# Attention masks of three branches added by identity products on TensorE, for the first half of layer 0

## The chip, the cores and the metric

The kernel runs on one core of a Trainium2 chip. The metric is device time in microseconds of one launch of the whole program, as a median of several runs. The engines are named as in the profile: PE is TensorE's matmuls, PEld its weight loads, DVE is VectorE, ACT is ScalarE, POOL is GpSimd, SP issues the DMAs.

## The reference, cut to what matters

A trunk of two layers works on 1024 tokens of width 1024. Layer 0 mixes the tokens with a sparse attention in three branches (compressed keys, selected keys, a window of 512) and with a grouped attention over a window of 128; layer 1 has a dilated attention. Each layer ends in a gated feed-forward block. All attentions are causal, and what a query may not see is masked before the softmax:

```python
s = jnp.einsum('bhgqd,bhkd->bhgqk', qr_b, kw) * SCALE
s = jnp.where(wmask, s, -jnp.inf)
o_win = jnp.einsum('bhgqk,bhkd->bhgqd', jax.nn.softmax(s, axis=-1), vw)
```

With 16 blocks chosen out of 16, the selected branch sees every key up to the query.

## The kernel before

**Stages.** The program is one long static order for each engine. The dense work (projections, output and feed-forward products) is a list of jobs over tokens 0 to 511 and 512 to 1023; the attentions of each half and layer are lists of units that are threaded between the dense products. This gives four phases of attention: layer 0 first half, layer 0 second half, layer 1 first and second half. The change touches the first of the four; in it each of 8 heads has a branch of kind `B` (window 128), `A` (selected) and `W` (window 512), and one of kind `cmp`.

**The order.** `run` (L377) is a list scheduler written out in the kernel: every task tells which engine it wants next, the task that could start earliest by a modelled clock of each engine goes first, and ties go by priority. `account` (L295) holds the modelled costs. So an operation that is left out moves everything behind it, as far as the modelled clocks move. `attend` (L1868) holds the units back to the pace of the dense work, and lets one through early where the dense product would have to wait.

**A unit.** `s_issue` (L1534) and `maxima` (L1555) first find each query's greatest score: PE products into a bank `pS`, a masked maximum on DVE (an instruction with the mask `mB` or `mW` and an accumulator read), the maxima `MR`, a transpose of `MR` on PE, a copy by ACT to `NM`, and a DMA that puts the row under the query tile. Then `st_unit` (L1613) makes the scores again, transposed, in a bank `pT` (two of these banks exist): for each block of keys two products with four-byte operands, of the same width, in one accumulation. `weights` (L1678) adds the masks on DVE (`pT<-pT,tDE`), takes the exponential on ACT (`S<-pT`), copies it to 16 bits on ACT (`PH<-S`), and subtracts the copy on DVE or POOL to get the low part (`PH<-S,PH`). `pv_unit` (L1700) multiplies both parts with the values (`pO<-S,PH`).

**Which masks.** `mask_ops` (L1640) returns the DVE additions of a unit. A head of kind `B` has two units, of 512 and 384 columns, with three additions (512, 256 and 128 columns); a head of kind `A` or `W` has three units with three additions (128, 256 and 128 columns). `tDE` holds the two triangles, `identB` a 128x128 identity, both in 16 bits. `st_unit` already has the other way, which the setting `ADD` (L58) switches on for each half by the letters of the kinds:

```python
nc.tensor.matmul(st.t[0:kp, o:o + w], a, qa, start=True, stop=False)
if br.get("add"):
    for x, _, kind in br["maskT"](j, bl):
        nc.tensor.matmul(st.t[:, o + x:o + x + P], self.identB, self.tDE[:, kind], start=False, stop=False)
nc.tensor.matmul(st.t[0:kp, o:o + w], b, qb, start=False, stop=True)
```

and `mask_ops` begins with `if br.get("add"): return []`. Every matmul goes through one helper, so the profile gives nearly all work the line L242, and the tiles tell it apart.

Of the kernel before, what the change touches and what calls it, by code (L numbers as in the profile page):

```python
# [54 lines left out]
BEGIN = 700.0  # L55
LEAD = 12000.0
PACE = (0.94, (0.0, 0.85), (0.0, 0.95), (0.0, 0.95))
ADD = ('', '')  # L58
STORE = 1
MM = 213.0  # L60

# [197 lines left out]
class Kernel:  # L259
# [1696 lines left out]
    def branches0(self, h):  # L1956
# [46 lines left out]
        for br in brs:  # L2003
            br["add"] = br["kind"] in ADD[h]
        if h == 0:
# [690 lines left out]
```

## Time and profile before

| | |
|---|---|
| median of 3 runs | 2660.91 us (2660.48 to 2662.5) |
| the profiled execution | 2661.24 us |
| its span, first to last instruction | 2659.2 us |
| PE busy in the span | 2555.7 us (96%) |
| DVE busy | 1882.5 us (71%) |
| ACT busy | 1356.3 us (51%) |
| POOL busy | 728.1 us (27%) |

The span is 2.0 us shorter than the time of that execution, and that execution 0.3 us longer than the median. PE is busy almost without a gap from 500 us on; what idle time it has lies ahead of that. A time that PE saves in the first 500 us is therefore saved at the end, since behind it the order is a queue of products, and a product that is added anywhere is paid at the end unless it fits into a gap.

### The profile page before, as it was taken

The numbers are of one execution on the slowest core, as the hardware profiler recorded it, in microseconds if no ns is written. First come the engines' busy times: TensorE is split into PE (matmuls) and PEld (weight loads), VectorE is DVE, ScalarE is ACT, GpSimd is POOL, SyncE is SP. The second block draws the span as 40 slices with busy tenths as digits, with TensorE's granted clock in tenths as the row PEclk, the third lists the DMA queues.
The fourth block names the chain that finished last, engine by engine and source line by source line (L and its number), as shares of the span: only waits on it lengthen the run. The fifth ranks groups of instructions, "written<-read, shape, count | busy, mean of one in ns | idle before, by whom it ended". The sixth has DMA issues, their size and how long they took to land. (4 is left out here: it accounts for less than half of the span.)

```text
span 2659.2 us, 42231 instructions
## 1 busy us (share of the span) xinstructions
PE 2555.7 (96%) x15446; PEld 1712.2 (64%) x15446; DVE 1882.5 (71%) x4266; ACT 1356.3 (51%) x2303; POOL 728.1 (27%) x513
## 2 busy tenths in 40 slices
PE   8988889999999999999999999999999999999998
PEld 7767768655555688765555688776666667654445
DVE  6888988877777775586666576687777775655554
ACT  7456555566666554344444454355556555433332
POOL 4444643210111446540000345341011114500002
PEclk9989999999999999999999999999999999999999
DMA  8665574233432345834444457954555544533320
GB/s 242 208 175 151 161 243 143 68 100 101 109 99 76 100 149 172 251 93 123 115 123 123 133 170 201 247 146 110 142 147 148 133 124 131 175 106 100 103 71 33
DMA packets 445939, 368.71 MB, mean 139 GB/s; under 512 B 54182, under 2 KB 383782, under 8 KB 445732
## 3 DMA queue, kind: packets, MB, share of 16 engines
q1 hardware_dynamic: 445732, 366.01, 48.7%
q8 instruction: 122, 2.00, 0.3%
q14 instruction: 85, 0.70, 0.1%
HBM read 298.80 MB, written 62.68 MB: 136 GB/s over the span
## 5 line engine op out<-in xcount | busy, mean ns | idle before, releaser
L242 PE MATMUL pD<-S,S 128*128 128x512 f16 (+3 forms) x9648 | 2177.5, 378 | 22.6 <-DVE S L242 15.9
L242 PEld LDWEIGHTS <-S 128*128 128x128 f16 x5376 | 509.3, 100 | 586.0 <-issue 42.3
L242 PEld LDWEIGHTS pD<-S,S 128*128 128x128 f32 x4272 | 729.3, 191 | 140.7 <-DVE S L242 5.8
L242 POOL TENSOR_TENSOR S<-S,S 128x512 f32<-128x512 f32 (+3 forms) x279 | 516.4, 1864 | 839.7 <-ACT S L242 716.4
L242 ACT ACTIVATE S<-pT 128x512 f32<-128x512 f32 (+3 forms) x304 | 171.6, 566 | 356.7 <-DVE pT L242 321.3
L242 ACT CAST S<-S 128x512 fp32r<-128x512 f32 (+2 forms) x283 | 274.1, 1020 | 154.9 <-DVE S L242 59.7
L242 DVE SCALAR_TENSOR_TENSOR S<-S,wsc,S 128x1024 f16<-128x1024 f32 x224 | 298.8, 1334 | 63.1 <-ACT S L242 62.3
L242 ACT ACTIVATE S<-S 128x1024 f16<-128x1024 f32 (+3 forms) x269 | 210.8, 784 | 142.5 <-DVE S L242 137.8
L242 ACT ACTIVATE S<-S,wsc 128x1024 f16<-128x1024 f32 x224 | 253.7, 1142 | 53.8 <-DVE wsc L242 48.5
L242 DVE TENSOR_TENSOR S<-S,S 128x512 fp32r<-128x512 f32 (+4 forms) x163 | 221.7, 1370 | 57.3 <-ACT S L242 55.1
L242 PE MATMUL pT<-S,S 128*128 128x128 f32 (+11 forms) x1072 | 255.1, 365 | 6.0 <-DMA S<-NM 3.6
L242 DVE SCALAR_TENSOR_TENSOR S<-pD,SM,S 128x512 f32<-128x512 f32 x208 | 156.2, 751 | 139.9 <-PE pD L242 130.3
L242 DVE TENSOR_TENSOR S<-pD,S 128x512 f32<-128x512 f32 (+1 forms) x238 | 156.5, 666 | 109.0 <-PE pD L242 90.8
L242 PEld LDWEIGHTS pT<-S,S 128*128 128x128 f32 (+2 forms) x1072 | 202.7, 230 | 35.9 <-DMA S<-NM 4.9
L242 DVE TENSOR_TENSOR PH<-S,PH 128x512 f16<-128x512 f32 (+3 forms) x235 | 173.6, 741 | 39.5 <-ACT PH L242 37.8
L242 POOL TENSOR_TENSOR PH<-S,PH 128x512 f16<-128x512 f32 (+2 forms) x69 | 83.4, 1210 | 418.8 <-ACT PH L242 338.3
L242 ACT ACTIVATE S<-pD,SM 128x512 f32<-128x512 f32 (+2 forms) x136 | 80.6, 605 | 200.8 <-PE pD L242 176.8
L242 ACT CAST PH<-S 128x512 f16<-128x512 f32 (+3 forms) x304 | 177.2, 587 | 10.5 <-PE pO L242 3.0
L242 PEld LDWEIGHTS <-PH 128*128 128x128 f16 (+1 forms) x3384 | 123.5, 99 | 52.8 <-issue 20.1
L242 DVE TENSOR_TENSOR pT<-pT,S 128x128 f32<-128x128 f32 (+4 forms) x176 | 91.8, 525 | 78.3 <-PE pT L242 77.5
L242 PE MATMUL pO<-S,PH 128*128 128x65 f16 (+1 forms) x3192 | 131.0, 195 | 10.6 <-DVE PH L242 8.8
L242 PE MATMUL pS<-S,S 128*128 128x256 f32 (+4 forms) x460 | 127.5, 366 | 6.6 <-DVE SM L242 3.4
(175 smaller groups left out, 1782.9 us busy)
## 6 DMA issues: line engine op xcount, KB each, us to landing
S<-in_w_gate_up SPq DMA_DIRECT2D x176, 512.0 KB
S<-in_w_down SPq DMA_DIRECT2D x88, 512.0 KB
S<-in_w_qkv_o SPq DMA_DIRECT2D x48, 512.0 KB
S<-in_w_in_e SPq DMA_DIRECT2D x22, 512.0 KB
xd<-S SPq DMA_DIRECT2D x32, 256.0 KB
S<-dhq SPq DMA_DIRECT2D x64, 128.0 KB
S<-in_w_out_e SPq DMA_DIRECT2D x16, 512.0 KB
S<-xd SPq DMA_DIRECT2D x32, 256.0 KB
```

The lines of the kernel that those rows point to most:

```text
L242: return fn(*a, **kw)
```

## The change

One setting:

```diff
-ADD = ('', '')
+ADD = ('BAW', '')
```

The first entry is for the first half of layer 0. There 72 DVE additions go (8 of 512 columns, 24 of 256, 40 of 128), and 120 pairs of a weight load of `identB` and a 128-column product of it with a triangle come in on PE: seven for each head of kind `B`, four for each of `A` and `W`. The `cmp` branch and the second half keep their additions on DVE. ACT and SP have as many instructions as before; DVE and POOL change by a few subtractions that the scheduler deals out otherwise.

On PE, a unit pair of kind `A` stood like this before (`S_118` is the query tile, `S_119` the keys, `pD` dense products):

```order
L242 MATMUL pS_2067<-S_129_1872,S_118_1660 128x384
L242 MATMUL pS_2067<-S_129_1872,S_118_1660 128x128
L242 MATMUL pT_2072<-S_118_1660,S_119_1664 128x512 x2
L242 MATMUL pT_2077<-S_118_1660,S_119_1664 128x384 x2
L242 MATMUL pT_2077<-S_118_1660,S_119_1664 128x128 x2
L242 MATMUL pD_1945<-S_68_879,S_130_1924 128x512 x2
```

and stands like this now:

```order
L242 MATMUL pT_2136<-S_118_1705,S_119_1709 128x512
L242 LDWEIGHTS identB
L242 MATMUL pT_2136<-tDE,identB 128x128
L242 MATMUL pT_2136<-S_118_1705,S_119_1709 128x512
L242 MATMUL pT_2140<-S_118_1705,S_119_1709 128x384
```

Each product with a triangle stands between the two score products of its block.

On DVE, behind the last operation that both kernels share (an addition out of `pD_1135`), these rows stood where the first unit of kind `B` begins:

```order
L242 TENSOR_TENSOR pT_1292<-pT_1292,tDE 128x512
L242 TENSOR_TENSOR pT_1302<-pT_1302,tDE 128x256
L242 ISA junk,SM_1320<-pS_1316,mB 128x256
L242 ISA SM_1320 128x1
L242 TENSOR_TENSOR pT_1302<-pT_1302,tDE 128x128
```

and now, four rows of maxima behind the same operation, stand these:

```order
L242 ISA junk,SM_1330<-pS_1326,mB 128x256
L242 ISA SM_1330 128x1
L242 TENSOR_TENSOR PH_1324<-S_33_1322,PH_1323 128x512
L242 TENSOR_TENSOR PH_1340<-S_34_1338,PH_1339 128x384
L242 ISA junk,SM_1330<-pS_1332,mB 128x128
```

The additions are gone, and the subtraction for the first weights (`PH_1324`) has moved up; before, other work stood between.

On PE again, the first weighted sum (`pO_1382`, weights `PH`) stood two dense groups, into `pD_1343`, behind the score products of the second head:

```order
L242 MATMUL pT_1360<-S_94_1161,S_86_1122 128x256 x2
L242 MATMUL pT_1360<-S_94_1161,S_86_1122 128x128 x2
L242 MATMUL pD_1343<-S_13_264,S_89_1139 128x512 x2
L242 MATMUL pD_1343<-S_13_264,S_90_1140 128x512
L242 MATMUL pD_1343<-S_14_283,S_89_1139 128x512 x2
L242 MATMUL pD_1343<-S_14_283,S_90_1140 128x512
L242 LDWEIGHTS PH_1339
```

and now stands one dense group behind them:

```order
L242 MATMUL pT_1360<-S_94_1161,S_86_1122 128x128
L242 MATMUL pD_1197<-S_23_360,S_99_1244 128x512 x2
L242 MATMUL pD_1197<-S_23_360,S_100_1245 128x512
L242 LDWEIGHTS PH_1323
L242 MATMUL pO_1382<-S_70_911,PH_1323 128x65
```

The scheduler has moved the weighted sums nearer to their scores. Over the units of this phase that can be matched by name (66 of 72), the products between a unit's last score product and its first weighted sum had 12,600 columns in the mean before and have 10,500 now. Where the units stand against the dense work has hardly moved: the first at 160 thousand dense columns in both, the 60th at 350 thousand in both, and from the second half's units on the two orders agree in this.

## Rows read from the trace of the kernel before

**Rows 1.** Windows by stretch: us, busy time (xinstructions) of each engine, granted clock, DMA.
```profile
core 0: us, PE busy (x) PEld busy (x) DVE busy (x) ACT busy (x) POOL busy (x), PEclk, DMA share, GB/s
111.00:350.00 239.00, 209.25 (x1602) 170.10 (x1601) 215.05 (x517) 143.39 (x279) 118.69 (x85) 0.92 0.63 178
350.00:500.00 150.00, 137.41 (x905) 107.86 (x906) 131.26 (x318) 82.81 (x154) 60.33 (x41) 0.95 0.51 151
500.00:900.00 400.00, 398.49 (x2764) 230.28 (x2763) 304.87 (x824) 256.17 (x437) 58.05 (x52) 1.00 0.35 94
900.00:1000.00 100.00, 96.79 (x700) 81.70 (x701) 80.02 (x157) 58.66 (x95) 44.85 (x31) 1.00 0.44 141
```

**Rows 2.** Waits of PE, 111 to 350 us: us in total, times, longest us.
```profile
PE pS L242 <- DVE MR L242: 14.0, 6, 4.9
PE pO L242 <- DVE PH L242: 3.6, 2, 1.9
PE pT L242 <- DMA S<-NM: 3.2, 2, 2.9
...
PE pS L242 <- DVE SM L242: 1.2, 3, 0.7
```

**Rows 3.** Waits on either side of the additions, same stretch, ACT's and DVE's.
```profile
ACT S L242 <- DVE pT L242: 39.6, 30, 2.8
...
DVE pT L242 <- PE pT L242: 13.5, 16, 2.1
```

**Rows 4.** The additions: instructions with `tDE`, DVE and POOL in the stretch, then shapes.
```profile
111.00:350.00 239.00, 26.79 (x72) 0.00 (x0) 0.92 0.63 178
```
```profile
L242 DVE TENSOR_TENSOR pT<-pT,tDE x72: 277/300/700, 112.6 to 319.1; 128x128 f32<-128x128 f32 x40, 128x256 f32<-128x256 f32 x24, 128x512 f32<-128x512 f32 x8
```

**Rows 5.** Timeline of DVE around three additions: start us, us, instruction.
```profile
121.31 0.66 DVE L242 TENSOR_TENSOR pT<-pT,tDE 128x512 f32<-128x512 f32 x1
121.89 0.21 DVE L242 TENSOR_SCALAR SM<-SM,vsc 128x4 f32<-128x4 f32 x1
122.02 0.42 DVE L242 TENSOR_TENSOR pT<-pT,tDE 128x256 f32<-128x256 f32 x1
122.35 0.41 DVE L242 CUSTOM_DVE_ANT_0 junk<-pS,mB 128x256 bf16<-128x256 f32 x1
...
122.69 0.29 DVE L242 TENSOR_TENSOR pT<-pT,tDE 128x128 f32<-128x128 f32 x1
122.91 0.42 DVE L242 CUSTOM_DVE_ANT_0 junk<-pS,mB 128x256 bf16<-128x256 f32 x1
```

**Rows 6.** Timeline of PE: 16-bit products of 65 columns, and transposes by an identity.
```profile
117.86 0.82 PE L242 MATMUL pO<-S,PH 128*128 128x65 f16 x21
118.52 0.36 PE L242 MATMUL pS<-S,S 128*128 128x256 f32 x1
```
```profile
130.47 0.60 PE L242 MATMUL pS<-ident,S 128*128 128x128 f32 x4
130.82 0.43 PE L242 MATMUL pS<-S,S 128*128 128x256 f32 x2
```

**Rows 7.** Timeline of PE at two of its waits (in brackets), and DVE before the second.
```profile
138.84 0.39 PE L242 MATMUL pO<-S,PH 128*128 128x65 f16 x7 [1.88 <-DVE PH L242]
```
```profile
214.71 0.27 PE L242 MATMUL pS<-ident,MR 128*4 128x128 f32 x1 [3.39 <-DVE MR L242]
```
```profile
208.34 5.32 DVE L242 TENSOR_TENSOR S<-S,S 128x512 fp32r<-128x512 f32 x3
213.58 0.28 DVE L242 CUSTOM_DVE_ANT_0 junk<-pS,mW 128x128 bf16<-128x128 f32 x1
```

**Rows 8.** Windows of ten us where the clock was low, columns as in rows 1.
```profile
140.00:150.00 10.00, 8.83 (x29) 7.49 (x30) 9.11 (x20) 3.21 (x6) 5.58 (x3) 0.50 0.45 161
190.00:200.00 10.00, 6.71 (x36) 5.83 (x36) 7.65 (x25) 5.97 (x12) 1.73 (x2) 0.55 0.82 164
...
240.00:250.00 10.00, 10.00 (x83) 8.37 (x83) 9.67 (x19) 7.62 (x14) 5.18 (x5) 0.72 0.76 239
```

## The prediction

> **What bounds the kernel now.** I read the windows by stretch first. From 500 to 900 us PE is busy 398.5 of 400 us, so the second half of layer 0 and what follows is a queue of products, and what PE loses or gains ahead of it arrives at the end unchanged [rows 1]. The change acts from 112.6 us, its first addition, to 319.1 us, its last [rows 4]; I take 111 to 350 us as its stretch. There no engine is full: PE 209.25 of 239 us (88%), DVE 215.05 (90%), ACT 143, POOL 119, and the granted clock is 0.92 [rows 1]. So PE is idle 239 - 209.25 = 29.75 us, and its clock gives away 239 x 0.08 = 19 us more. These two sums are all that a relief of DVE can win.
>
> Next the waits. Of the 29.75 us, 14.0 are PE's transposes of the maxima, waiting for DVE (`MR`, six times, up to 4.9 us), 4.8 wait for DVE's subtractions and small sums (`PH`, `SM`), 3.2 for a DMA [rows 2]; the rest is spread over ACT and smaller things. DVE in turn waits for PE's scores 13.5 us, always in front of an addition, and ACT waits 39.6 us for additions [rows 3]. The reader is to see two engines, each about nine tenths busy, which wait for each other in a fixed order, and that the additions lie in the middle of both waits.
>
> **What is removed.** 72 additions with 26.79 us of busy time [rows 4]. Back to back they cost less, since the next instruction starts before the row of the addition ends: 121.31 to 121.89 is 0.58 us for 512 columns, 122.02 to 122.35 is 0.33 for 256, 122.69 to 122.91 is 0.22 for 128 [rows 5]. Then 8 x 0.58 + 24 x 0.33 + 40 x 0.22 = 4.6 + 7.9 + 8.8 = 21.3 us of DVE's time. With the additions go DVE's waits in front of them, 13.5 us [rows 3], though the next DVE operation may then wait itself. DVE's load in the stretch falls from 215 to about 194 us.
>
> **What is added.** 120 pairs of a 16-bit weight load and a product of 128 columns on PE; the trace of before has none of them. From below: 21 pairs of a 16-bit load and a 65- or 64-column product start within 118.52 - 117.86 = 0.66 us, 31 ns a pair [rows 6]; 63 more columns at 2.4 GHz are 26 ns, so 57 ns a pair and 6.8 us in all. From above: four transposes with four-byte loads take 130.82 - 130.47 = 0.35 us, 87 ns each [rows 6], or 10.5 us; and since the four-byte load of the next score product can hide only under a short product, I allow 97 ns, 11.6 us. I take 75 ns, nearer to the 16-bit row since the load is of its kind: 9.0 us. At the clock of the stretch (16% of it at 1.2 GHz, which the mean of 0.92 means, and there a product takes twice as long) that is 9.0 x 1.16 = 10.4 us. There is no case below nothing here, because PE is the engine that ends the kernel and the pairs stand in its order.
>
> Beside this row stands the Trainium skill, "TensorE: Matmul & The Clock Gate", section "Back-to-back issue gap": a sustained stream of load and product pairs of 128 columns takes about 81 ns each. By that the pairs would come to an estimated 9.7 us; no row of this trace shows such a pair, and the sum keeps its 9.0.
>
> **What lies beside other work.** A part of the 10.4 us falls where PE would have waited anyway. The 120 pairs against the 13 waits of PE in the rows [rows 2] are about nine for each wait, 0.7 us, and a wait that is left and longer than that swallows them: with a handful of such waits I take 3 us as hidden. If every wait went, nothing would be hidden and the whole 10.4 us would be paid.
>
> **Which waits go.** The `PH` and `SM` waits, 4.8 us: PE stood 1.88 us at 138.84 behind a DVE that had had no gap for over 20 us [rows 7]; 21.3 of 239 us is 9%, so such a run held about 1.8 us of additions. These go. The `MR` waits, 14.0 us, have other roots: the one of 3.39 us at 214.71 comes behind three subtractions that took 5.32 us, without an addition among them [rows 7]. I take a third of the 14.0 as gone, 4.7 us. DMA, ACT and unnamed waits stay. Together 9.5 us. The scheduler takes some of that back: it knows that the additions are gone and puts the weighted sums 12,600 - 10,500 = 2,100 columns nearer to their scores, 0.9 us at 2.4 GHz. Against that a unit spares its addition and its turn in DVE's queue, and ACT's wait for an addition was 39.6 / 30 = 1.3 us [rows 3]. So the two nearly cancel for one unit's path, and what is left is that DVE has less to do. I take 2 us off: 7.5 us.
>
> **What the clock gives back.** The trace shows low clock behind PE's waits: 0.50 from 140 to 150 us, right behind the wait of 1.88 us; 0.55 from 190 to 200 us; 0.72 from 240 to 250 us [rows 7, 8]. In these three windows (1 - clock) x 10 is 5.0, 4.5 and 2.8 us of the 19. The first goes with its waits. The second contains the DMA wait of 2.9 us [rows 2] and stays. Of the third and of the remaining 7 us, I count a fifth, 2 us. Sum 7 us; the bounds are 0 and 19.
>
> **The sum.** +10.4 - 3 - 7.5 - 7 = -7.1 us, say 7 to 8. Against the profiled execution of 2661.24 us (its span 2659.2 and 2.0 around it, 0.3 above the median of the runs) that gives 2653.5, and as a median 2653 us. Behind 350 us nothing changes: the units of the second half stand at the same dense columns as before, and their additions stay on DVE.
>
> **The rivals.** One: *VectorE alone binds the stretch.* Then the stretch shrinks by the whole 21.3 us: 2661 - 21 = 2640 us. For it: DVE at 90% beside PE at 88%; and from 900 to 1000 us, where DVE has 80%, PE is idle only 3.2 of 100 us and its clock is 1.00 [rows 1]. With 194 us of work in 218 us, DVE would be at 89% again. Against it: PE's own 209 us plus 10 make 219, so it would need a full queue on PE, or the clock to come back. The Trainium skill, "Perfetto Trace Analysis", section "Identifying the Most-Contended Engine", judges TensorE not by its busy time but by its weight loads' share and calls the engine with the highest occupancy the one to relieve. By that rule PE has 170.10 of 239 us, 71%, and DVE is that engine; the trace bears it out only halfway, since PE's products leave no more than 12% free.
>
> Two: *The waits move, and price and gain cancel.* Relief of DVE and added products meet at 10 us each, the clock stays where it is: 2661 us. For it: the longest waits follow subtractions, which stay.
>
> Three, slower: *The scheduler spends the relief.* PE's consumers were moved up by as much as the units' path got shorter; DVE runs late against the order because of its long subtractions, not because of the additions, and so PE waits as long as before. Then PE pays the 10.4 us in full: 2671 us, up to 2674 with the upper price. The point from which it decides is PE's idle time in the stretch: if it stays above 27 us, this is what happens. For it: rows 7, and the moved sums in the order. Against it: 21 us less work for an engine that was 90% busy.
>
> That the change doesn't do what it says is excluded by the order: 72 additions are gone and 120 pairs are there.
>
> **How the numbers follow.** My forecast (2653, its own range 2646 to 2660) has 0.42, rival one (2634 to 2646) 0.22, rival two (2656 to 2666) 0.17, rival three (2665 to 2675) 0.19. About 0.2%, 5.3 us, is what a measurement of this kernel can tell from no change: faster means below 2655.6, slower above 2666.2. From the forecast 0.30 is faster and 0.12 the same; rival one is faster; rival two the same but for 0.02 on each side; rival three is slower with 0.15 and the same with 0.04. Together 0.54 faster, 0.29 the same, 0.17 slower. The range reaches to 2637 and to 2669; it leaves out about 0.07 of rival one and 0.12 of rival three.
>
> **What would show it.** In the profile of the changed kernel: no `tDE` operation on DVE before the second half; the products with `identB`, 57 to 97 ns apart from their neighbours; a stretch of about 232 us from the first score products to the last unit of `cmp`, with DVE near 84% and PE at 91% or more; PE's waits for `PH` and `SM` almost gone, those for `MR` near 9 us; no window at 0.50 near 140 us. Wrong would be: PE's idle time unchanged (rival three), pairs over 100 ns (the price), or a clock in the stretch still at 0.92 with shorter waits (the clock term).

## The result, and the profile after

The changed kernel is slower, by 0.75%: 2683.05 us, median of four runs (2675.6 to 2685.2), against 2661.7 us for the kernel before (2660.48 to 2663.37). The ratio is 1.0075, with a 95% interval from 1.0054 to 1.0095. The forecast was 2653 us, the range 2637 to 2669; both the sign and the range were wrong. The profiled execution took 2685.2 us.

First the page's span line and its line of busy times, of the kernel after:

```profile
span 2683.2 us, 42404 instructions
PE 2569.3 (96%) x15566; PEld 1715.5 (64%) x15566; DVE 1866.3 (70%) x4197; ACT 1354.9 (50%) x2303; POOL 724.2 (27%) x510
```

PE's busy time rose by 13.6 us over the 2555.7 of before; the span grew by 24.0. Next the windows by stretch, which answer to [rows 1], with two shorter ones that the reading needs:

```profile
core 0: us, PE busy (x) PEld busy (x) DVE busy (x) ACT busy (x) POOL busy (x), PEclk, DMA share, GB/s
111.00:350.00 239.00, 213.62 (x1691) 166.98 (x1690) 196.91 (x443) 136.20 (x269) 109.49 (x78) 0.95 0.58 169
350.00:500.00 150.00, 131.08 (x819) 105.40 (x818) 125.35 (x283) 79.03 (x145) 59.71 (x40) 0.91 0.59 169
500.00:900.00 400.00, 398.26 (x2767) 229.51 (x2766) 310.30 (x849) 257.54 (x442) 58.31 (x54) 1.00 0.32 88
325.00:425.00 100.00, 83.40 (x504) 66.09 (x503) 78.38 (x182) 45.37 (x88) 39.23 (x30) 0.88 0.73 213
246.00:292.00 46.00, 38.08 (x281) 29.46 (x279) 34.21 (x73) 23.39 (x44) 20.04 (x13) 0.93 0.33 109
```

The same two shorter stretches in the kernel before:

```profile
325.00:425.00 100.00, 88.78 (x577) 71.96 (x576) 87.52 (x211) 50.60 (x99) 44.28 (x29) 0.97 0.71 219
246.00:292.00 46.00, 45.38 (x370) 37.55 (x369) 40.64 (x108) 31.26 (x61) 25.69 (x19) 1.00 0.43 130
```

Read alone, the stretch of the change looks no worse: DVE has 196.9 of 239 us, PE's idle time is 25.4 us where it was 29.75, the clock 0.95 where it was 0.92. The loss is in two places inside and behind it. From 246 to 292 us PE idles 7.9 us (before 0.6), and from 325 to 425 us 16.6 us at a clock of 0.88 (before 11.2 at 0.97). To place it, I counted the dense products (into `pD`) in both traces (from 0) and compared the times at which each starts; the order of the dense work is the same in both:

| dense product | before, us | after, us | after minus before |
|---|---|---|---|
| 600th | 249.7 | 246.0 | -3.7 |
| 700th | 285.1 | 291.7 | +6.7 |
| 900th | 363.3 | 372.1 | +8.8 |
| 1000th | 402.8 | 420.3 | +17.5 |
| 2000th | 712.7 | 730.2 | +17.5 |
| 4000th | 1230.7 | 1254.6 | +23.9 |
| 9000th | 2512.1 | 2536.0 | +23.9 |

Up to the 600th product the change is ahead by 3.7 us. Between the 600th and the 700th it loses 10.4, between the 900th and the 1000th 8.7, between 900 and 1200 us some 6 more, and what is lost by then does not come back.

PE's waits from 111 to 350 us (us in total, times, longest), the answer to [rows 2]:

```profile
PE pS L242 <- DVE SM L242: 9.9, 6, 3.8
PE pS L242 <- DVE MR L242: 8.0, 8, 2.0
...
PE pO L242 <- DVE PH L242: 1.2, 1, 1.2
PE pT L242 <- DMA S<-NM: 1.0, 2, 0.6
```

The waits for `MR` and `PH` went down as forecast, by 6.0 and 2.4 us. But those for `SM`, which were to vanish, rose from 1.2 to 9.9. The instructions with `tDE`, which answer to [rows 4] (duration in ns: shortest, median, longest; first and last start):

```profile
L242 PE MATMUL pT<-tDE,identB x120: 219/230/330, 113.0 to 323.4; 128*128 128x128 bf16 x120
L242 DVE TENSOR_TENSOR pT<-pT,tDE x104: 273/300/700, 378.8 to 1005.4; 128x128 f32<-128x128 f32 x64, 128x256 f32<-128x256 f32 x32, 128x512 f32<-128x512 f32 x8
```

So the change does what it says: DVE adds no mask of the first half. And the longest wait of the stretch, at 275.37 us, first PE, then DVE and POOL ahead of it:

```profile
275.37 0.39 PE L242 MATMUL pS<-S,S 128*128 128x256 f32 x1 [3.78 <-DVE SM L242]
```

```profile
265.43 9.28 DVE L242 TENSOR_TENSOR S<-S,S 128x512 f32<-128x512 f32 x5
274.63 0.68 DVE L242 CUSTOM_DVE_ANT_0 junk<-pS,mW 128x512 bf16<-128x512 f32 x1
```

```profile
264.32 3.53 POOL L242 TENSOR_TENSOR S<-S,S 128x512 fp32r<-128x512 f32 x2 [6.75 <-ACT S L242]
269.25 1.20 POOL L242 TENSOR_TENSOR PH<-S,PH 128x512 f16<-128x512 f32 x1 [1.39 <-ACT PH L242]
270.68 2.95 POOL L242 TENSOR_TENSOR S<-S,S 128x1024 fp32r<-128x1024 f32 x1 [0.22 <-ACT S L242]
273.59 1.64 POOL L242 TENSOR_TENSOR PH<-S,PH 128x256 f16<-128x256 f32 x1
```

Five operations with both operands in SBUF take 9.28 us on DVE. The row merges them under the shape of the first; one by one they are two of 512 columns in plain f32 (1.01 and 2.05 us), two of 512 columns with a result in fp32r (1.09 and 2.08) and one of 1024 columns (3.37). With POOL empty, in the last run below, these three forms take 0.69, 1.05 and 1.22 us in the mean, which makes 4.7 for the five, about half. POOL is busy in 7.7 of these 9.3 us, and the masked maximum that PE waits for stands behind them. The custom instruction that reads `pS`, beside the same POOL, takes its usual 0.68.

### The profile page after: what moved, and what is told of

Its sections match the earlier page's. It is cut to its first block, busy times and chain, and to the rows that moved or that the text cites. A ratio compares the mean times of both kernels' runs of the same rounds, so it can differ in the third digit from the quotient of the medians.

```text
span 2683.2 us, 42404 instructions
## 1 busy us (share of the span) xinstructions
PE 2569.3 (96%) x15566; PEld 1715.5 (64%) x15566; DVE 1866.3 (70%) x4197; ACT 1354.9 (50%) x2303; POOL 724.2 (27%) x510
## 5 line engine op out<-in xcount | busy, mean ns | idle before, releaser
L242 PE MATMUL pD<-S,S 128*128 128x512 f16 (+3 forms) x9648 | 2184.6, 379 | 29.5 <-DVE S L242 18.2
L242 PEld LDWEIGHTS <-S 128*128 128x128 f16 x5376 | 509.6, 100 | 588.2 <-issue 44.3
L242 PEld LDWEIGHTS pD<-S,S 128*128 128x128 f32 x4272 | 733.9, 193 | 147.4 <-DMA S<-mixd 7.7
L242 POOL TENSOR_TENSOR S<-S,S 128x512 f32<-128x512 f32 (+2 forms) x278 | 516.8, 1872 | 860.8 <-ACT S L242 729.1
L242 ACT ACTIVATE S<-pT 128x512 f32<-128x512 f32 (+3 forms) x304 | 170.6, 565 | 366.8 <-DVE pT L242 298.2
L242 ACT CAST S<-S 128x512 fp32r<-128x512 f32 (+2 forms) x283 | 273.4, 1019 | 153.2 <-DVE S L242 63.2
L242 DVE SCALAR_TENSOR_TENSOR S<-S,wsc,S 128x1024 f16<-128x1024 f32 x224 | 295.5, 1319 | 63.8 <-ACT S L242 61.8
L242 ACT ACTIVATE S<-S 128x1024 f16<-128x1024 f32 (+3 forms) x269 | 210.8, 784 | 142.4 <-DVE S L242 137.9
L242 ACT ACTIVATE S<-S,wsc 128x1024 f16<-128x1024 f32 x224 | 253.7, 1142 | 54.1 <-DVE wsc L242 48.5
L242 PE MATMUL pT<-S,S 128*128 128x128 f32 (+11 forms) x1072 | 263.7, 368 | 4.8 <-ACT S L242 3.8
L242 DVE TENSOR_TENSOR S<-S,S 128x512 fp32r<-128x512 f32 (+4 forms) x164 | 214.7, 1321 | 69.7 <-ACT S L242 68.2
L242 DVE SCALAR_TENSOR_TENSOR S<-pD,SM,S 128x512 f32<-128x512 f32 x208 | 156.2, 751 | 139.9 <-PE pD L242 130.6
L242 DVE TENSOR_TENSOR S<-pD,S 128x512 f32<-128x512 f32 (+1 forms) x238 | 156.7, 667 | 112.7 <-PE pD L242 98.6
L242 DVE TENSOR_TENSOR PH<-S,PH 128x512 f16<-128x512 f32 (+2 forms) x236 | 190.0, 810 | 48.5 <-ACT PH L242 46.5
L242 PEld LDWEIGHTS pT<-S,S 128*128 128x128 f32 (+2 forms) x1072 | 201.4, 227 | 31.9 <-ACT S L242 5.6
L242 POOL TENSOR_TENSOR PH<-S,PH 128x512 f16<-128x512 f32 (+3 forms) x68 | 81.7, 1201 | 391.4 <-ACT PH L242 315.5
L242 ACT ACTIVATE S<-pD,SM 128x512 f32<-128x512 f32 (+2 forms) x136 | 80.6, 605 | 208.8 <-PE pD L242 180.0
L242 ACT CAST PH<-S 128x512 f16<-128x512 f32 (+3 forms) x304 | 176.6, 587 | 12.5 <-PE pO L242 3.1
L242 PEld LDWEIGHTS <-PH 128*128 128x128 f16 (+1 forms) x3384 | 122.3, 98 | 51.0 <-issue 20.1
L242 DVE TENSOR_TENSOR pT<-pT,S 128x128 f32<-128x128 f32 (+4 forms) x176 | 91.7, 525 | 81.7 <-PE pT L242 80.8
L242 PE MATMUL pS<-S,S 128*128 128x256 f32 (+4 forms) x460 | 126.2, 364 | 12.8 <-DVE SM L242 8.3
L242 PE MATMUL pO<-S,PH 128*128 128x65 f16 (+1 forms) x3192 | 128.9, 194 | 8.8 <-DVE PH L242 8.2
```

Of the source, the lines that this page charges most:

```text
L242: return fn(*a, **kw)
```

## The experiments

The change does three things at once: it takes the additions from DVE, puts the pairs on PE, and makes the scheduler deal out another order. The runs with old or new order and with or without additions and pairs separate these. In them an operation can be reckoned by the scheduler and not issued, or issued and not reckoned, so that the rest of the order stays word for word the same. The edit, with three switches (`...` marks what is left out; the added lines move the helper from L242 to L243 and further in the rows of these runs):

```diff
 # st_unit
+    if PLAN:
+        self.account("p", "matmul", args, dict(start=False, stop=False))
+    if PAIRS:
+        nc.tensor.real.matmul(*args, start=False, stop=False)
 # weights, for a branch with the setting
+    if not PLAN:
+        yield "v"
+        self.account("v", "tensor_tensor", (v, v, tab), dict(op=ALU.add))
+        if ADDS:
+            nc.vector.real.tensor_tensor(v, v, tab, op=ALU.add)
 ...
         yield "a", self.room(S2=1, PH=2)
+        if br.get("add") and PLAN and ADDS:
+            for v, tab in mine:
+                nc.vector.real.tensor_tensor(v, v, tab, op=ALU.add)
```

`PLAN` off gives the order of before, on that of after.

**The work without the order.** Old order with pairs and without additions:

> The order of before, word for word, with the 72 additions taken off VectorE and the 120 identity products put onto TensorE; the scheduler still reckons as if the additions were on VectorE. Theory S (the scheduler spent the relief by moving work up): with the work where it was, the relief is kept and the time is 2650 to 2662 us, 20 us under the changed kernel. Theory P (the products' price is the loss and the relief is worth nothing in any order): 2672 us or more, with TensorE's idle time from 111 to 350 us still near 30 us.

Measured 2663.3 us (2659.18 to 2665.67, ten runs) against 2660.98; ratio 1.001 [1.0, 1.0019]. So the change without its new order is all but neutral, +2.3 us. That is 1.3 us above theory S's range and far below theory P's.

**The relief alone.** Old order, neither additions nor pairs; the masks of the three branches are left out, and the exponent is scaled down so that it stays finite:

> The order of before without the 72 additions and without the identity products: the masks of the three branches are left out in the first half of layer 0 (and the exponentials there are taken of scores divided by 1024, so that they stay finite). It prices the relief alone. Theory S: 10 us or more are won, 2651 us or less. Theory P: within 3 us of before, 2658 to 2664 us.

Measured 2658.31 us (2651.56 to 2662.93, ten runs); 0.9988 [0.9978, 0.9999], -2.7 us: in theory P's range. The relief is worth next to nothing in this order.

**The price alone.** Old order, additions and pairs, so that the masks are added twice:

> The order of before with the additions kept on VectorE and the 120 identity products added on TensorE, so that each mask is added twice. It prices the products alone. By the pitch of the pairs in the changed kernel's trace, 97 ns each at full clock, 11.6 us: 2672 us where nothing hides them. Theory S holds 2668 to 2674 us. If the price itself is the whole loss, 2680 us.

Measured 2667.63 us (2665.54 to 2673.05, five runs); 1.0031 [1.0018, 1.0044], +6.6 us. Relief and price add up to +4.0 where both together gave +2.3: additive within what can be measured.

Where on the way these differences arise, the profiled executions show, one of each run. So many us behind the kernel before do their dense products start:

| run | 1000th | 3500th | 3750th | 9000th |
|---|---|---|---|---|
| relief alone | +1.6 | +2.3 | -1.7 | -2.0 |
| price alone | +10.8 | +12.5 | +7.9 | +6.9 |
| both | +5.9 | +6.6 | +3.5 | +2.2 |

In the stretch itself the relief won nothing, and the pairs were paid nearly in full. Between the 3500th and the 3750th product (1090 to 1164 us in the kernel before) all three gain 3 to 5 us on it, where order and work are the same as in it. So what is lost ahead of 500 us does not arrive at the end quite unchanged, and PE's idle time does not all lie ahead of 500 us: of its 103 us in the kernel before, 47 lie behind. Why they gain there is not shown; a difference of 3 to 5 us at the end can't be laid to the stretch by the end alone.

Why is 21 us less DVE work worth so little? The window and PE's waits, 111 to 350 us, of the relief alone:

```profile
111.00:350.00 239.00, 210.39 (x1606) 172.57 (x1605) 199.93 (x450) 143.06 (x279) 120.79 (x86) 0.91 0.62 178
```

```profile
PE pS L243 <- DVE MR L243: 16.6, 6, 4.7
PE pO L243 <- DVE PH L243: 2.8, 3, 1.9
PE pT L243 <- DMA S<-NM: 2.7, 1, 2.7
PE pS L243 <- DVE SM L243: 2.7, 1, 2.7
```

DVE's busy time fell by 15 us, PE is as idle as before (28.6 us) and the clock as low (0.91). The waits for `MR` and `SM` did not shrink at all.

**The order without the work.** New order, additions still on DVE, no pairs; then new order with neither (the masks left out as above):

> The order of the changed kernel with the additions on VectorE and no identity products: what the moved order costs by itself. Theory S: the moved order is the harm, 2670 us or more, since VectorE has its additions back as well. Theory P: the order is harmless, 2659 to 2665 us.

Measured 2704.05 us (2695.72 to 2704.6, four runs); 1.0168 [1.0151, 1.0185], +43.1 us on the same work in the old order, as theory S has it. One thing sets this run apart: the additions have no place of their own in the new order, they are issued on DVE where the unit's exponential has its turn.

> The order of the changed kernel without additions and without identity products: the masks of the three branches are left out in the first half of layer 0 (and the exponentials there are taken of scores divided by 1024, so that they stay finite). Against the changed kernel it prices the products in the new order: at the price that they had in the old order, 6.6 us, 2675 us; at the 11.6 us of their pitch, 2670 us. If order, price and relief do not add up but act on each other, it lies outside 2667 to 2678 us.

Measured 2675.36 us (2673.16 to 2679.7, four runs); 1.0058 [1.0037, 1.0079]. Beside the relief alone in the old order (2658.31) this is the same work in another order: +17.0 us. That is the largest term of the change, and it stood in my sum with nothing. It is not a constant of the order: with the pairs it is 20 us (2683.05 - 2663.3), with the additions 43. Put the other way, the same relief that is worth 2.7 us in the old order is worth 28.7 in the new one (2704.05 - 2675.36), where the additions stand in places that nobody dealt them.

**Is it this order, or any other?** Two kernels with all the work of before, in which the scheduler reckons the 72 additions at 0.9 or 1.1 of their cost (`RECKON` multiplies the two numbers of `COST["v"]` for them), so that the order moves for no reason of the work:

> The work of the kernel before, every operation of it; only the scheduler reckons the 72 additions of the first half at 0.9 of their cost, which deals out the first half's order anew. Theory L: 2670 us or more though no work has changed. Theory M: the second half's maxima stand where they stood or later, so 2658 to 2665 us.

> As the run before, with the additions reckoned at 1.1 of their cost. Theory L: 2670 us or more. Theory M: the second half's maxima stand as in the kernel before, 2658 to 2665 us.

Measured 2672.37 us (1.0044 [1.0028, 1.006]) and 2666.89 us (1.0026 [1.0016, 1.0035]), against 2660.33. By its cost numbers (68 ns and 1.043 ns a column) that moves single operations by 20 to 60 ns in the reckoning, and it costs 6 to 12 us. The first of the two lies in theory L's range, the second between the two theories.

**Where in the order?** The second of the two places is where the second half's units begin: in the kernel after, the 33rd to 36th sets of maxima stand at 410, 423, 423 and 423 thousand dense columns, before at 423, 426, 431 and 449. A rule holds them back:

```diff
+                    if h == 1 and br["kind"] == "B" and self.done < HELD + 1000.0 * b:
+                        return INF
```

> The changed kernel, with one rule more in the scheduler: the score products of the second half's B heads may not start before the dense work has come as far as it had in the kernel before (about 170 us of dense products, one head per further 1 us). Theory M (the loss behind 320 us comes from the second half's units, which moved up beside the norms and gates of the dense work): 8 us or more come back, 2665 to 2674 us, and TensorE's idle time from 325 to 425 us falls from 16 to 10 us or less. Theory L (any other order than the one found for the kernel before costs this much, wherever it differs): 2675 to 2685 us, no gain.

Measured 2671.87 us (2669.97 to 2674.85, six runs); 1.0044 [1.0029, 1.0059]. From the 900th to the 1000th dense product it takes 40.6 us (before 39.5, after 48.2), from the 600th to the 700th 44.4 as in the kernel after (45.7). One place is mended by itself, and half of the loss comes back: theory M's time, though PE's idle time from 325 to 425 us falls from 16.6 to 13.9 only, not to 10. A third place goes with it. From the 2500th to the 3500th dense product (860 to 1090 us in the kernel before) the kernel after loses 9.3 us on the kernel before, the other runs in the same order (with additions, with neither, and with the fills below) 7.1, 6.3 and 7.3, the three runs in the old order 0.5 to 0.8, and this run 1.2.

Two hybrids change the reckoning at the 550th dense product, one from old to new, one from new to old, with the work of the kernel after (`PLAN` becomes a comparison of `self.done` with 117150):

> Work of the kernel after (identity pairs, no additions in the first half). The scheduler reckons the additions on DVE, as in the kernel before, until the 550th dense product, and the pairs on PE, as in the kernel after, behind it; so the order is that of the kernel before up to about 228 us. Theory P (the order's cost sits in two places, products 600 to 700 and 900 to 1000): the stretch from the 600th to the 700th dense product takes 35 to 38 us again (after: 45.7), the one from 900 to 1000 lies between 40 and 48 us since the second half's maxima stand between the two orders, and the time is 2664 to 2672. Theory D (the cost is spread, each unit that is moved up pays a little): half of it stays, 2670 to 2675, with 600 to 700 at 40 us or more.

Measured 2674.97 us (1.0046 [1.0033, 1.0058], five runs). The first place is well again, 37.1 us, and the second too, 35.9; but from the 700th to the 800th product, where neither parent loses, it takes 49.2 us against 40.3.

> The same work, and the reckoning of the kernel after until the 550th dense product, that of the kernel before behind it. Up to the 600th product the order is that of the kernel after. Theory P: what was dealt ahead of the switch already brings the loss of 600 to 700 (44 to 46 us), and of 900 to 1000 a part goes; 2673 to 2681. Theory D: 2670 to 2675, 600 to 700 near 40 us.

Measured 2669.11 us (1.0029 [1.002, 1.0038], ten runs), 41.2 us in the first place. Theory P falls in both runs, and theory D, which is near in the times, has the first hybrid's places wrong: the losses are not tied to fixed places, and not spread evenly. Each order that was dealt out anew (six of them) has its own, and all six are slower than the old order with the same work, by 6 to 20 us. (Additions forced into the new order, 43 us, are left out of this count.)

**What PE waits for.** The three longest waits for `MR` in the kernel before and the longest of the kernel after each end behind DVE operations with their operands in SBUF that took 1.7 to 14 times their own time. In the kernel before, 111 to 350 us, by form (count | busy us, mean ns):

```profile
L242 DVE TENSOR_TENSOR PH<-S,PH 128x512 f16<-128x512 f32 x34 | 27.2, 804 | 0.4
L242 DVE TENSOR_TENSOR S<-pD,S 128x512 f32<-128x512 f32 x35 | 23.5, 677 | 2.0 <-PE pD L242 2.0
L242 DVE TENSOR_TENSOR S<-S,S 128x512 fp32r<-128x512 f32 x15 | 22.9, 1555 | 1.4 <-ACT S L242 1.4
...
L242 DVE TENSOR_SCALAR MR<-SM 128x4 fp32r<-128x4 f32 x23 | 8.5, 373 | 0.2
```

The next run keeps the kernel before and takes POOL's reads away: from about 105 to 375 us each of its two-input operations becomes a fill of the same tile, so what POOL computes there is left out.

```diff
+            if key == "g" and name.startswith("tensor_") and NOREAD[0] <= k.done < NOREAD[1]:
+                out = kw["out"] if "out" in kw else a[0]
+                return self.real.memset(f(out), 0.001)
             return fn(*a, **kw)
```

> The kernel before with one thing left out: between about 105 and 375 us of its time each two-input operation of POOL (sums, products, subtractions of the low parts) is replaced by a fill of the same tile with a constant, so POOL writes and does not read, and is done sooner. Order on PE, DVE, ACT and SP word for word that of the kernel before. In the kernel before DVE operations with operands in SBUF are stretched in the stretch 111 to 350 us: a 128x512 sum takes 1.56 us in the mean there and 0.68 at its shortest, the 128x4 scaling to MR 0.37 and 0.14; together some 35 us of DVE's 215. Theory W (what PE waits for are these stretched operations, which the removed additions left as they were): the sums come to 0.7 to 1.1 us, MR to 0.17, DVE to 180 to 190 us, PE's waits for MR fall from 14 us below 5, and the time to 2638 to 2650. Theory V (a static order gives no more back for these than for the additions): waits for MR stay above 10 us and the time is 2653 to 2660. Rival to both: the operations are as long without POOL's reads, then nothing moves, 2659 to 2663.

Measured 2632.24 us (2627.26 to 2634.42, four runs); 0.9888 [0.9871, 0.9905]: 27 us faster than the 2659.25 beside it, with DVE's instructions and their order unchanged. At the 1000th dense product its trace is 25.7 us ahead, so the gain does arise here. The same forms, and the window and waits of 111 to 350 us:

```profile
L247 DVE TENSOR_TENSOR PH<-S,PH 128x512 f16<-128x512 f32 x34 | 23.1, 685 | 0.1
L247 DVE TENSOR_TENSOR S<-S,S 128x512 fp32r<-128x512 f32 x15 | 15.3, 1061 | 3.7 <-ACT S L247 3.7
L247 DVE TENSOR_SCALAR MR<-SM 128x4 fp32r<-128x4 f32 x24 | 6.5, 271 | 0.2
```

```profile
111.00:350.00 239.00, 221.99 (x1756) 183.97 (x1756) 197.05 (x575) 154.10 (x303) 46.17 (x96) 0.95 0.70 200
```

```profile
PE pT L247 <- DMA S<-NM: 5.8, 3, 3.0
PE pS L247 <- DVE MR L247: 2.2, 2, 1.5
```

The waits for `MR` are 2.2 us instead of 14.0. Theory W holds in what it says of the waits: they came from DVE's stretch beside POOL, which the additions left as it was. Its sizes were off: the time is below its range, DVE's busy time is 197 us, not 180 to 190, and the scaling to `MR` takes 0.27 us, not 0.17. The two-operand sums are as short here (1.06 us), beside a POOL that writes, as in the last run below with POOL empty (1.05); the scaling, which takes 0.16 there, is still stretched. A part of the 27 us may be POOL's being sooner done (a fill of 512 columns takes 0.74 us, a sum 1.6 to 1.8). In the kernel before ACT waited 2.5 us for POOL in the stretch, PE's products and DVE for none of it; no run takes away the reads and keeps POOL's pace.

> The same fill instead of POOL's two-input operations, and the edit's work in the order of the kernel before: identity pairs on PE, no additions on DVE in the first half. Beside the run without the fill (2663) it tells what the change would do where DVE's operations are not stretched. Theory W: 2642 to 2655, within +2 to +8 us of the run with the additions and the fill, since PE then waits for little and the pairs' 6.6 to 11.6 us are paid nearly in full. Theory V: 2656 to 2663.

Measured 2637.9 us (2633.55 to 2638.4, five runs); 0.9909 [0.9893, 0.9925]. Without the stretch the pairs cost 5.7 us more than the additions, as theory W had it for the difference; the time is below its range.

**What the new order is made of.** The kernel after with the same fills:

> The kernel after with POOL's two-input operations of 105 to 375 us replaced by fills of the same tile, as in the two runs before; the order on PE and DVE is word for word that of the kernel after. It tells what the 17 us of the new order are made of. Theory Q (the new order costs because it deals PE's transposes behind DVE operations that are stretched beside POOL, five subtractions in 9.28 us among them): without the stretch the two orders come out within 5 us of each other, 2636 to 2643, beside 2637.9 for the old order with the same work and fill. Theory R (the cost lies in the distances that the new order leaves, whatever DVE's operations take): 10 to 20 us of it stay, 2648 to 2658.

Measured 2647.93 us (2640.18 to 2651.71, six runs); 0.9941 [0.9928, 0.9955]. The new order now costs 10 us over the old one (2637.9), where it cost 20 without the fills: at the edge of theory R's range, and outside Q's. The six runs spread over both, and the profiled one, 2641.31, is among the quick ones; the median alone does not decide. The two places part here: from the 600th to the 700th dense product it takes 34.6 us where the kernel after took 45.7, and the old order with the fills 36.3; from the 900th to the 1000th 44.3 against 38.2. The windows of that kernel:

```profile
246.00:292.00 46.00, 45.70 (x367) 36.96 (x362) 34.87 (x91) 32.72 (x56) 9.68 (x18) 1.00 0.52 160
325.00:425.00 100.00, 87.67 (x552) 72.33 (x552) 73.53 (x198) 49.65 (x92) 25.04 (x21) 0.93 0.69 204
```

In the first place the whole loss was the stretched burst (theory Q); in the second 6.1 us of it stay, with DVE busy only 74%, and so does the third, 7.3 (theory R).

**A version that is faster.** Nothing is left out here: the order of before, with POOL's two-input operations of 105 to 375 us issued on DVE, at the place the order gives them, first with pairs, then with additions:

```diff
+            if key == "g" and name.startswith("tensor_") and ONDVE[0] <= k.done < ONDVE[1]:
+                return getattr(k.nc.vector.real, name)(*a, **kw)
             return fn(*a, **kw)
```

> Nothing is left out here. The order of the kernel before, pairs on PE and no additions on DVE in the first half, and POOL's two-input operations of 105 to 375 us issued on DVE at the place that the order gives them. DVE gives up 72 additions (21 us by pitch) and the stretch beside POOL (some 35 us), and takes about 97 operations of POOL, at 0.7 us about 55 us with the wide ones. Theory W' (it is POOL's reads that make the gain of 27 us, and the relief can pay for taking them over): 2640 to 2655, faster than the kernel before. Theory X (DVE, in one queue, waits for inputs that POOL waited for by itself, 118 us of waits in front of POOL's operations in the profile): 2670 to 2700.

Measured 2650.78 us (2646.99 to 2657.11, five runs); 0.9963 [0.995, 0.9976]: faster than both kernels.

> The same move of POOL's operations to DVE in the kernel before, additions still on DVE, no pairs. DVE's load in 105 to 375 us would be 238 - 35 + 55, some 258 of 270 us. Under both theories it is slower than the run with the pairs, by more than 10 us, if DVE is the engine that binds then; if it comes out faster than that run, the relief is worth less than the pairs' price even on a DVE that is full.

Measured 2657.34 us (2654.48 to 2662.39, eleven runs); 0.9985 [0.9976, 0.9993]. The windows, with pairs, then with additions:

```profile
111.00:350.00 239.00, 219.68 (x1772) 173.88 (x1773) 215.98 (x560) 147.38 (x288) 1.67 (x1) 0.96 0.64 183
```

```profile
111.00:350.00 239.00, 207.98 (x1607) 167.22 (x1608) 226.75 (x609) 141.62 (x276) 1.68 (x1) 0.95 0.61 172
```

POOL is all but empty, and DVE has its work as well. The kernel with the additions comes out 4.8 us under the one before, but not by the stretch: at the 1000th dense product its trace is 2.0 us behind that of before, and it gets ahead only between the 3500th and the 3750th, where the runs in the old order above gain too. So in the stretch DVE took over 92 operations and lost 2 us by it; most of what they cost was won back from the stretched ones. These two runs do not tell the stretch from POOL's being sooner done. The waits for `MR` are still 8.4 us with the pairs and 9.8 with the additions, since DVE is about as full as before: it stands at 90% with the pairs and at 95% with the additions. With the pairs the trace is 6.9 us ahead at the 1000th product, and here, for the first time in the old order, the pairs are the cheaper way, by 6.6 us (more than 10 were expected). Theory W' has the time right; theory X, by which DVE's one queue would wait for POOL's inputs, falls.

## Why the prediction was wrong

**The waits that go, and the clock (the step of the 7.5 and the 7 us): wrong.** They were to bring 14.5 us; the relief alone brought 2.7, none of it by the 1000th dense product, at a clock of 0.91 where it had been 0.92. I had seen the clue: [rows 7] has PE's wait of 3.39 us behind three subtractions of 5.32 us, and I wrote that the wait had another root, then let a third of the `MR` waits go all the same. I did not ask why they take 2.41, 2.40 and 0.68 us there, when their form takes 1.05 in the mean with POOL empty. Each of the two long ones ends 0.93 us behind an operation of POOL (210.75 behind 209.82, 213.07 behind 212.14); these are POOL's two, merged:

```profile
208.10 4.04 POOL L242 TENSOR_TENSOR S<-S,peTv 128x512 f32<-128x512 f32 x2
```

The longest wait of all, 4.95 us, shows it most plainly; kernel before, PE, then DVE, then POOL:

```profile
299.86 0.37 PE L242 MATMUL pS<-ident,MR 128*4 128x128 f32 x1 [4.95 <-DVE MR L242]
```

```profile
297.49 0.18 DVE L242 RECIPROCAL SM<-OS 128x4 f32<-128x4 f32 x1
297.58 2.23 DVE L242 TENSOR_SCALAR MR<-SM 128x4 fp32r<-128x4 f32 x1
```

```profile
297.32 2.46 POOL L242 TENSOR_TENSOR S<-S,S 128x1024 fp32r<-128x1024 f32 x1 [1.31 <-ACT S L242]
```

A scaling of four columns, 0.16 us in the median, lasts 2.23 us, and ends 0.03 us behind POOL's sum (297.58 + 2.23 = 299.81 and 297.32 + 2.46 = 299.78). The Trainium skill, "SBUF — State Buffer", section "Who interferes with whom", has the rule: a DVE instruction with two inputs in SBUF contends with a GpSimd instruction that reads SBUF, one in a two-port mode (a `tensor_scalar` can be) with any, and the one that comes second stands still until the first has ended. This trace agrees, and the run with the fills shows what it is worth here, up to 27 us. The additions have one operand in `pT`, outside SBUF, and lasted 0.28 to 0.35, 0.39 to 0.43 and 0.66 to 0.70 us by their width: they were never the stretched ones. Taking them away made DVE idle, not early. In the old order with the pairs DVE has 192 of 239 us, and its wait for `pS` alone is 18.4 us, where the additions' waits for `pT` had been 13.5 [rows 3].

**"Behind 350 us nothing changes": wrong, and the largest miss.** I gave the re-dealt order no term beyond 2 us, since the first and the 60th unit stood at the same dense columns. The second half's 33rd to 36th sets of maxima did not, though I had read the two orders as agreeing from there on, and that place alone costs 8.7 us. The order costs 17 us with the masks left out in both (2675.36 - 2658.31) and 20 us with the pairs (2683.05 - 2663.3). With it the sum closes along this way: 6.6 - 2.7 + 17.0 = 20.9, measured 21.4. In the traces the new order with the pairs is 11.6 us behind the old one at the 1000th dense product and 21.7 at the 9000th, so nearly half of its cost lies behind that.

**The price: near at the end, by luck in part.** 10.4 us less 3 hidden are 7.4; at the end the pairs cost 6.6 us in the old order and 7.7 in the new one (2683.05 - 2675.36). But on PE they cost more than I took: from a first score product of 128 columns to what follows the second, 173 ns pass without a pair between (kernel before) and 249 with one (kernel after); over all widths it is about 97 ns a pair at full clock, the upper bound (11.6 us for 120). And waits did not hide 3 us of it: the run with the price alone is 10.8 us behind at the 1000th product, and what is missing at the end comes back behind 1090 us.

**The rivals.** The second, that price and gain cancel at 2661, is what the work does in the old order (+2.3). The third had the sign, 2671 to 2674, but not the reason: its point was PE's idle time in the stretch above 27 us, and that was 25.4. It asked whether the order spends the relief; the order lost more than there was to spend, in part behind the stretch. The first, that DVE alone binds, would have brought 2640 us; the relief alone, without any price, stayed at 2658. The four pairs of runs side by side, with DVE's busy time from 111 to 350 us in the one with additions:

| DVE with additions, of 239 us | additions, us | pairs, us | pairs minus additions |
|---|---|---|---|
| 197 (old order, POOL fills) | 2632.2 | 2637.9 | +5.7 |
| 215 (old order: before) | 2661.0 | 2663.3 | +2.3 |
| 227 (old order, POOL's work on DVE) | 2657.3 | 2650.8 | -6.6 |
| 198 (new order) | 2704.1 | 2683.1 | -21.0 |

In the old order the sign of the trade turns somewhere between 90% and 95% of DVE, in kernels that differ in POOL's work too. In the new order it is the other way at 83%, with the additions in forced places. So DVE's fullness alone does not set the sign. The rule of the busiest engine, which I set beside the first rival (the Trainium skill, "Perfetto Trace Analysis", section "Identifying the Most-Contended Engine"), would have DVE relieved in the second row already; the run says no.

**The signs.** No `tDE` on DVE before the second half: right. Pairs at 57 to 97 ns: at the upper end in the mean. PE at 91% or more: no, 89%. DVE near 84%: 82%. `MR` waits near 9 us: 8.0. `SM` waits gone: no, 9.9. No window at 0.50 near 140 us: right, 0.83. A stretch of 232 us: no, the last pair stands at 323.4 us where the last addition stood at 319.1. Most of these are right and the time is wrong by 30 us, since none of them looked at the order behind the stretch.

What stays open: why the second place still costs 6 us with the fills, and by which wait the third costs its 6 to 9. That it goes when the second half's units are held back is shown; which of them matters is not.

## What to carry to other kernels

Before an engine is relieved, look at what the waits end in: an instruction that lasts far beyond its usual duration can point to what is contended, and removing healthy work beside it freed idle time only. In a statically scheduled kernel a change of work is also a change of order; price the order by itself (reckon without issuing), because re-dealing a tuned one cost 6 to 20 us here, several times what the work was worth. The same trade can have either sign: in one order the pairs on PE lost 2 to 6 us, and won 6.6 once DVE had POOL's work as well.

## What the runs showed of the hardware that I had not expected

Four columns can take as long as a thousand: the scaling to `MR` lasted from 0.10 to 2.35 us between 111 and 431 us of the kernel before, and all 16 scalings to `MR` over 0.4 us in the kernels before and after, in that stretch, end 0.02 to 0.03 us behind an operation of POOL; reciprocals of the same size stayed at 0.15 to 0.18 in the kernel before. The stretch cost DVE nearly as much as POOL's work itself: when DVE took it over, 92 operations more from 111 to 350 us, the mean of its 128x512 operations with two SBUF operands and an fp32r result fell from 1.56 to 1.05 us, that of the scaling from 0.37 to 0.16, and its busy time rose by only 12 of 239 us (kernel before against the run with additions and POOL's work on DVE).
